# One DMA queue for loads and stores in a strided mean-subtract kernel: SyncE issues both in alternation, ScalarE none

## The chip, the cores and the metric

The kernel runs on one core of one Trainium2 chip. Time is device microseconds of the whole execution, and the states of runs are compared only where they are the same; all runs told here were of the fast state. A single-core program has no second die to compare with, so "fast" means that no run was over 1.5% above the fastest of its kernel. Shorter times are better; a difference under 2% counts as the same.

## The reference

```python
def reference(x):                      # x: 8 x 4096 x 2112, float32
    B, S, D = x.shape
    stride = 4
    x_r = x.reshape(B, S // stride, stride, D)
    pooled = x_r.mean(axis=2)
    upsampled = np.repeat(pooled, stride, axis=1)
    return (x - upsampled).astype(np.float32)
```

Each group of four rows loses its own mean. 276.8 MB are read and as many written; there is little arithmetic per byte.

## The kernel before

Four rows of 2112 numbers make one partition's row of 33,792 bytes, 128 of them a tile of 4.325 MB, and there are n = 64 tiles. Six tiles fit in SBUF (`SLOTS = 6`). SyncE issues all loads into its DMA queue, ScalarE all stores into another; VectorE adds three times and subtracts once per tile.

```python
    with tc.tile_critical():
        for k in range(n):
            b, lap = k % SLOTS, k // SLOTS
            load = nc.sync.dma_start(out=slots[b][:], in_=xg[k * P:(k + 1) * P])
            if lap:
                load._wait_ge(store_sems[b], 16 * lap)
            load.then_inc(load_sems[b], 16)

        with nc.vector.Fori(0, laps) as lap:
            landed = nc.vector.to_reg(16 * lap + 16)
            for b in range(SLOTS):
                reduce_tile(b, landed)      # three adds, one multiply-add; waits on load_sems[b]
            # ... (step semaphore wound back)
        # ... (the rest of the tiles)

        for k in range(n):
            b = k % SLOTS
            store = nc.scalar.dma_start(out=og[k * P:(k + 1) * P], in_=slots[b][:])
            store._wait_ge(done_sem, k + 1)
            store.then_inc(store_sems[b], 16)

    for k in range(n - SLOTS, n):           # closing waits on the last stores
        total = nc.gpsimd.to_reg(16 * (k // SLOTS + 1))
        tc.keep_in_program_order(nc.gpsimd.wait_ge(store_sems[k % SLOTS], total))
```

## Time and profile before

| | before |
|---|---|
| timed, median of the first 3 runs | 1284.73 us (1284.65 to 1285.19) |
| span of the profiled execution | 1283.3 us |
| VectorE busy | 1026.5 us, 80% |
| the 16 DMA engines busy | 50.1% loads + 50.0% stores of the span |
| first load landed, last store landed (semaphore records) | 13.30 and 1282.39 us |

The lines themselves, and how to read them, stand in the prediction below.

### The profile page before, as it was taken

What the parts mean: (1) busy time and instruction counts of PE and PEld (TensorE: products, weight loads), DVE (VectorE), ACT (ScalarE), POOL (GpSimd) and SP (SyncE); (2) the same over time, 40 slices, a digit from 0 to 9 for tenths busy, and PEclk for the clock granted to TensorE, in tenths of its full rate; (3) what the DMA queues carried; (4) which work ended last, traced back from release to release, by engine and by line L of the source; (5) the groups of instructions that cost most, each with busy time, mean ns of one, the idle gap of its engine ahead of it and who ended that gap; (6) DMA issues with size and microseconds to landing.
All of it is one profiled execution on the core that took longest, in us unless ns stands there. A gap on an engine that the chain in (4) does not pass through costs nothing.

```text
span 1283.3 us, 483 instructions
## 1 busy us (share of the span) xinstructions
DVE 1026.5 (80%) x256; POOL 0.2 (0%) x4
## 2 busy tenths in 40 slices
DVE  5998788787887877878778787787877878878785
POOL 0000000000000000000000000000000000000000
DMA  9999999999999999999999999999999999999999
GB/s 404 420 436 429 434 437 434 427 437 436 427 436 437 434 427 437 436 427 436 437 433 428 437 436 426 437 437 433 428 437 434 428 437 437 432 429 437 434 427 404
DMA packets 18432, 553.66 MB, mean 431 GB/s; under 512 B 2048, under 2 KB 2048, under 8 KB 2048
## 3 DMA queue, kind: packets, MB, share of 16 engines
q1 hardware_dynamic: 9216, 276.83, 50.1%
q10 hardware_dynamic: 9216, 276.83, 50.0%
HBM read 276.82 MB, written 276.82 MB: 431 GB/s over the span
## 4 chain that ended last, share of the span: by engine, by line
DVE 73%; another core or an unknown queue 24%; DMA 1%; issue 1%; DVEq 0%; SPq 0%
DVE slot L69 38%; DVE s_ps L63 18%; DVE s_sb L63 18%; DMA slot<-in_x_dram 1%; DVEq L90 0%; SPq L133 0%; SPq L82 0%
## 5 line engine op out<-in xcount | busy, mean ns | idle before, releaser
L69 DVE SCALAR_TENSOR_TENSOR slot<-s_sb,slot 128x8448 f32<-128x8448 f32 x32 | 286.7, 8958 | 1.1
L69 DVE SCALAR_TENSOR_TENSOR slot<-s_ps,slot 128x8448 f32<-128x8448 f32 x32 | 286.6, 8957 | 1.1
L63 DVE TENSOR_TENSOR s_sb<-slot 128x2112 f32<-128x2112 f32 x32 | 75.5, 2358 | 123.7 <-DMA slot<-in_x_dram 123.7
L63 DVE TENSOR_TENSOR s_ps<-slot 128x2112 f32<-128x2112 f32 x32 | 75.7, 2367 | 112.1 <-DMA slot<-in_x_dram 112.1
L63 DVE TENSOR_TENSOR s_ps<-s_ps,slot 128x2112 f32<-128x2112 f32 x64 | 151.4, 2366 | 2.2
L63 DVE TENSOR_TENSOR s_sb<-s_sb,slot 128x2112 f32<-128x2112 f32 x64 | 150.9, 2358 | 2.2
L122 POOL MEMSET const-bfloat16-1.0<- 128x1 bf16 x1 | 0.1, 102 | 0.0
L122 POOL MEMSET const-uint8-127<- 128x1 uint8 x1 | 0.1, 102 | 0.0
L122 POOL MEMSET const-float32-0.0<- 128x1 f32 x1 | 0.1, 99 | 0.2 <-issue 0.2
L122 POOL MEMSET const-float32-1.0<- 128x1 f32 x1 | 0.1, 99 | 0.0
## 6 DMA issues: line engine op xcount, KB each, us to landing
slot<-in_x_dram SPq DMA_DIRECT2D x64, 4224.0 KB, 60.1
out_dram<-slot ACTq DMA_DIRECT2D x64, 4224.0 KB, 43.5
```

The costliest lines, as they stand in the source:

```text
L63: add = nc.vector.tensor_add(out=s[:], in0=first, in1=rows[:, f, :])
L69: sub = nc.vector.scalar_tensor_tensor(out=rows, in0=s[:, None, :].to_broadcast([P, STRIDE, D]), scalar=-1.0 / STRIDE, in1=rows, op0=mybir ...
L122: nc = _bacc.Bacc("TRN2", target_bir_lowering=False, num_devices=1)
```

## The change

The intent is to have one queue whose order is fixed by the program: a load and a store in turn, so that the loads cannot crowd out the stores. Because SyncE stops at a load whose buffer is not yet free, one store more than needed (`AHEAD = 1`) is put in front of each such load, so that the queue still holds work meanwhile.

```diff
+AHEAD = 1
@@
-        for k in range(n):
+        def load_tile(k):
             b, lap = k % SLOTS, k // SLOTS
             load = nc.sync.dma_start(out=slots[b][:], in_=xg[k * P:(k + 1) * P])
             if lap:
                 load._wait_ge(store_sems[b], 16 * lap)
             load.then_inc(load_sems[b], 16)
+
+        def store_tile(k):
+            b = k % SLOTS
+            store = nc.sync.dma_start(out=og[k * P:(k + 1) * P], in_=slots[b][:])
+            store._wait_ge(done_sem, k + 1)
+            store.then_inc(store_sems[b], 16)
+
+        for k in range(SLOTS):
+            load_tile(k)
+        for k in range(n):
+            store_tile(k)
+            if k >= AHEAD and k + SLOTS - AHEAD < n:
+                load_tile(k + SLOTS - AHEAD)
@@ (the loop of stores on ScalarE is gone)
-        for k in range(n):
-            b = k % SLOTS
-            store = nc.scalar.dma_start(out=og[k * P:(k + 1) * P], in_=slots[b][:])
-            store._wait_ge(done_sem, k + 1)
-            store.then_inc(store_sems[b], 16)
```

## The prediction

> **What bounds the kernel now.** I read the page first, its parts 1 to 3, to see which resource is full; then the DMA queue's own waits, to see who holds whom; then the DMA view and the windows, to get the cost of one transfer with one queue alone and with both. The page of the kernel before:
>
> ```profile
> span 1283.3 us, 483 instructions
> DVE 1026.5 (80%) x256; POOL 0.2 (0%) x4
> ...
> DMA packets 18432, 553.66 MB, mean 431 GB/s; under 512 B 2048, under 2 KB 2048, under 8 KB 2048
> ...
> q1 hardware_dynamic: 9216, 276.83, 50.1%
> q10 hardware_dynamic: 9216, 276.83, 50.0%
> ...
> slot<-in_x_dram SPq DMA_DIRECT2D x64, 4224.0 KB, 60.1
> out_dram<-slot ACTq DMA_DIRECT2D x64, 4224.0 KB, 43.5
> ```
>
> VectorE is busy 1026.5 us, so it is idle a fifth of the time: 16.04 us of work per tile, 64 tiles. The two DMA queues take 50.1% and 50.0% of the 16 engines' whole span, together all of it. So the transfers set the end. There are 128 of them (64 loads, 64 stores) of 4224 KB, that is 128 partitions of 33,792 bytes, 4.325 MB each. The chain of waits on the page names VectorE with 73%, which must not mislead: its pieces are VectorE working while a transfer that VectorE then waits for is under way.
>
> The waits confirm it. The loads wait in SyncE for stores (the DMA queue's own waits; columns: total us, times, longest), and VectorE's idle time goes to loads (the engines' waits):
>
> ```profile
> SPq L85 <- DMA out_dram<-slot: 1169.0, 58, 50.7
> ```
>
> ```profile
> DVE s_sb L63 <- DMA slot<-in_x_dram: 123.7, 30, 13.3
> DVE s_ps L63 <- DMA slot<-in_x_dram: 112.1, 30, 3.8
> ```
>
> A load waiting in the sequencer costs nothing as long as other transfers are queued, and they are: a load takes 60.1 us from issue to landing, a store 43.5. At some 20 us for one load and one store side by side, there are always about three loads and two stores under way.
>
> Next, is the DMA slower with two queues than with one? Windows of the kernel before (columns: window and its length, VectorE and GpSimd busy with counts, clock, DMA share, GB/s), then the DMA view of a stretch in which only loads run:
>
> ```profile
> 54.78:1252.66 1197.88, 969.27 (x241) 0.00 (x0) 1.00 1.00 433
> ```
>
> ```profile
> q1 hardware_dynamic: 352, 10.81, 100.2%
> ```
>
> In the long middle, from 54.78 to 1252.66 us (the landings of the loads of tiles 3 and 63, as the semaphore records have them), 60 tiles' loads and 60 stores land: 1197.88 / 120 = 9.982 us for one transfer. In the loads-only stretch from 4 to 29 us the one queue fills the engines alone (100.2%) and moves 10.81 MB in 25 us, 433 GB/s, the same rate. The counts there are coarse, so I take landings. The first two loads land at 13.30 and 23.25 us by the semaphore records: 9.95 us between them. At the end only stores are left; the last three are issued at 1228.93, 1248.87 and 1268.88 and take 33.5, 23.5 and 13.5 us to land, so they land at 1262.4, 1272.4 and 1282.4: 9.97 to 9.98 us each. One queue alone, back to back, runs at 9.95 to 9.98 us per transfer; two queues at 9.98.
>
> **What the Trainium skill says.** "DMA: Bandwidth & Descriptors", section "Where 436 GB/s comes from", gives 435.2 GB/s as the ceiling of the 16 ports. From it I estimate 4.325 MB / 435.2 = 9.94 us as the least time of a transfer; the trace's 9.95 to 9.98 agrees and leaves 0.4% to gain at most. The same page, "Issuing engines are not separate DMA queues", says that DMAs of all issuing engines run on the same 16 engines, and that several issuers save only sequencer time. The trace agrees: one queue alone 433 GB/s, both 433. Its section "Queues, rings and completion order" says that an engine goes round-robin between queues packet by packet, and within one queue consumes in order. The trace fits: with both queues filled each has half the time. "Anatomy of one DMA — SWDGE (gpsimd) path" says that semaphore waits sit on the issuing sequencer, while the DMA engines just consume. This makes a wait at the head of one sequencer hold back everything behind it, and is what the change risks.
>
> **The change, part by part.** Bytes, transfers, VectorE's work and slots stay as they are. ScalarE's 64 issues (338 ns each in the trace) move to SyncE, whose own 64 take 328 ns: 64 x 0.338 = 21.6 us more sequencer time spread over 1283 us, beside transfers that are already queued; nothing on the path.
>
> What changes is the order. The queue now holds: six loads, store 0, store 1, load 6, store 2, load 7, and so on; load k+5 stands between stores k and k+1, and waits for store k-1 to land. I work it out with 9.96 us a transfer (the mean of 9.95 and 9.97). Loads 0 to 5 are issued within 3.9 us and land at 13.3, 23.3, 33.2, 43.2, 53.1, 63.1. Store 0 is issued when VectorE is done with tile 0, at 29.5, but stands behind load 5: it lands at 73.1, store 1 at 83.0. At 73.1 load 6 is issued, and behind it store 2 (VectorE was done with tile 2 at 61.5), while store 1 is under way. At 83.0 load 7 and store 3 (done at 77.5) follow. From then on, when store k-1 lands, load k+4 and store k are still to run: 20 us of work. Load k+5 comes with a delay of under a microsecond, and store k+1 follows it at once, if VectorE is done with tile k+1. Load k+1 landed five transfers, 50 us, before that moment; VectorE needs 16. So neither wait ever empties the queue: 20 us of reserve on the loads, some 34 on the stores.
>
> At the end load 63 is the 123rd transfer, landing at 13.3 + 122 x 9.96 = 1228.4, where it was 1252.7. VectorE is then done at about 1244.5 instead of 1268.9; stores 59 to 62 are already queued, and store 63 queues behind them.
>
> The sum: first landing 13.3 (0.95 of start and 12.35 of the first load, as now), 127 more at 9.96 = 1264.9, last landing 1278.2, plus 0.95 from the last landing (1282.4) to the end as now: span 1279.2. The timed figure is 1.4 us above the profiled span (1284.73 against 1283.3): 1280.6. Before, the same formula needs 9.993 us a transfer, for the 1269.1 us from first to last landing: 0.03 x 127, some 4 us, is all there is to win. Changing from load to store inside a ring may cost a few hundredths of a microsecond, so I say 1281.
>
> **The rivals.** First, a bubble at each change of direction: every transfer now follows one of the other kind in the same ring. If the completion of a store or the start of a load held up its successor, that would happen up to 122 times; 0.2 us each gives 24 us, 1305 and slower by nearly 2%, a full microsecond 1400. Against it: loads follow loads and stores follow stores at 9.95 to 9.98 without a bubble, and with two queues each engine already serves loads and stores in turn at 9.98. For it: no stretch of the kernel before has a load behind a store in one queue. I hold this for the main risk, about one in twenty for losses over 2%.
>
> Second, blocking at the head of SyncE: a store that is ready stands behind a load that waits. Were the reserve too short, the queue would run dry for part of 20 us per tile; 2 us per tile would make 1410. The working above leaves 20 us of reserve; the extra store ahead is there for just that. Few per cent.
>
> Third, a gain: loads come at full rate instead of in halves, so VectorE starts tile 1 on with data earlier and finishes 24 us earlier. But the end is that of the last store, and the bytes before it are the same; even at the 9.94 estimate the timed end is about 1278. Faster by 2% (under 1259) would need 442 GB/s; nothing in the trace shows it.
>
> **Range and chances.** Central 1281. The low end, 1276, is a little under 9.94 us a transfer; the high end, 1288, allows 0.06 us more per transfer than computed. Within 2%: 0.93; slower 0.05 for the first two rivals; faster 0.02.
>
> **What would show it.** One DMA queue with 18432 packets at about 100%, mean 432 to 433 GB/s with no slice under 400 beyond the first and last. Loads from 6 on take about 30 us from issue to landing (three transfers), stores about 40 (four). SyncE's waits are nearly all on stores, 58 times, close to 19.3 us each (two transfers less two issues), and hardly any on VectorE after the first two stores. VectorE's last instruction ends near 1244.5, with about the same total busy time. I am wrong if the middle shows over 10.1 us per transfer with full queues (first rival), if the DMA share falls below 97% with SyncE waiting for VectorE or for landings (second), or if the rate in the middle exceeds 436 GB/s.

## The result, and the profile after

The changed kernel took 1287.99 us (median of 5 runs, 1287.80 to 1288.35); the kernel before, in the same rounds, 1284.73 (1284.56 to 1285.19). The ratio is 1.0024, with a 95% interval of 1.0012 to 1.0037. Ratios here are the mean time of one kernel's runs over that of the other's of the same rounds, so not quite the ratio of the medians. So the time is the same within 2%, and still 3.3 us longer, clear of the noise, where the prediction's centre was nearly 4 us shorter than before.

The page of the changed kernel, the same parts as in the prediction:

```profile
span 1286.0 us, 481 instructions
DVE 1026.0 (80%) x256; POOL 0.2 (0%) x4
...
q1 hardware_dynamic: 18432, 553.66, 99.9%
...
slot<-in_x_dram SPq DMA_DIRECT2D x64, 4224.0 KB, 29.9
out_dram<-slot SPq DMA_DIRECT2D x64, 4224.0 KB, 39.5
```

One queue now carries everything and fills the engines for 99.9% of the span. A load takes 29.9 us from issue to landing (three transfers), a store 39.5 (four): the queue is as deep as worked out. What SyncE waits for (total us, times, longest us):

```profile
SPq L86 <- DMA out_dram<-slot: 1111.3, 58, 28.5
SPq L93 <- DVE slot L70: 85.5, 5, 25.7
```

The 58 waiting loads wait 19.2 us each on the average, and while they do the engines are busy. Of the five waits for VectorE, two are those of stores 0 and 1 and lie in the first 130 us (41.4 us together), and the others come at the end, where stores follow each other with no load between them and earlier stores are still queued.

So the queue is never empty, and yet time is lost. Where, the windows show (window and its length, VectorE and GpSimd busy with counts, clock, DMA share, GB/s). I cut at landings of the changed kernel: of the first load (13.36), of the fifth (53.29), and at 216.80, the landing of the 21st transfer. The changed kernel:

```profile
13.36:53.29 39.93, 39.59 (x12) 0.00 (x0) 1.00 1.00 433
53.29:216.80 163.51, 152.12 (x37) 0.00 (x0) 1.00 1.00 428
216.80:1240.00 1023.20, 823.05 (x207) 0.00 (x0) 1.00 1.00 433
```

The kernel before, in the same windows:

```profile
13.36:53.29 39.93, 39.62 (x12) 0.00 (x0) 1.00 1.00 420
53.29:216.80 163.51, 138.74 (x34) 0.00 (x0) 1.00 1.00 433
216.80:1240.00 1023.20, 823.17 (x208) 0.00 (x0) 1.00 1.00 433
```

After 217 us both run at 433 GB/s. The kernel before loses in the first window, into which its first store falls (issued at 29.5 us); the changed kernel loses in the second, where its queue first changes from loads to stores and back. The DMA share stays 1.00 in both: the engines are not idle, single rows take longer.

The trace records each row (33,792 bytes by one engine) with its start and duration. The views of the profile do not print these records; I read them from the packed trace. They do not name the engine, but in a filled queue each row starts within some 10 ns of the end of the one before it, so they can be chained into 16. Nearly every row, load or store, in both kernels takes 1251 ns. In the changed kernel the last rows of load 5, begun at 60 to 62 us, just ahead of the queue's first store, are longer: 0.92 us more per engine, mean of the 16. After that single rows are longer here and there up to about 260 us, most of them (39 of 59) the last row of a load ahead of a store, others among a load's first three; 0.84 us more on the mean, but 2.6 us on the slowest engine. In the kernel before there is one such place, at 31 to 37 us, where its first store begins, with 0.99 us per engine, and nothing after it. So both kernels pay nearly the same at their first store, with one queue or two; what one queue adds is the longer rows after it.

A transfer has landed when its slowest engine has. The 16 landings of one transfer lie within 0.43 us of each other at load 4, and within 3.2 to 3.5 us in the whole later part, where six engines follow ten by about 1.1 us or more. To compare runs I use one sum: from the first to the last landing, less 127 transfers of 9.983 us. (9.983 is the changed kernel's own pace once the losses are over: landing 27 at 276.79, landing 128 at 1285.06, 1008.27 / 101.) This "lost" time is 1269.09 - 1267.84 = 1.2 us before and 1271.70 - 1267.84 = 3.9 us after. The 2.6 us between them are the whole difference of the profiled spans (1286.0 - 1283.3 = 2.7).

### The profile page after: what moved, and what is told of

Same layout as the page of the kernel before. It is cut to its first block, busy times and chain, and to the rows that moved or that the text cites. A ratio compares the mean times of both kernels' runs of the same rounds, so it can differ in the third digit from the quotient of the medians.

```text
span 1286.0 us, 481 instructions
## 1 busy us (share of the span) xinstructions
DVE 1026.0 (80%) x256; POOL 0.2 (0%) x4
## 3 DMA queue, kind: packets, MB, share of 16 engines
q1 hardware_dynamic: 18432, 553.66, 99.9%
## 4 chain that ended last, share of the span: by engine, by line
DMA 93%; DVE 4%; SPq 1%; issue 0%
DMA out_dram<-slot 89%; DMA slot<-in_x_dram 3%; DVE slot L70 2%; DVE s_ps L64 1%; SPq L86 1%; DVE s_sb L64 1%; SPq L141 0%; SPq L83 0%
## 6 DMA issues: line engine op xcount, KB each, us to landing
slot<-in_x_dram SPq DMA_DIRECT2D x64, 4224.0 KB, 29.9
out_dram<-slot SPq DMA_DIRECT2D x64, 4224.0 KB, 39.5
```

## The experiments

Theory: the loss is a one-off. It is paid at changes from load to store inside one ring (the list of work of one queue) while the engines make that change in step (at the same moment), and fades as they drift apart; it has to do neither with waiting, nor with SyncE, nor with VectorE. Rivals: a reserve in the queue that is a little too short; SyncE as the issuer; VectorE's traffic in the same memory; a small cost on every transfer.

All my kernels have one edit in common. The closing waits stand inside the critical section and wait on constants. One run is the control for that.

**Control.**

```diff
-    for k in range(n - SLOTS, n):
-        total = nc.gpsimd.to_reg(16 * (k // SLOTS + 1))
-        tc.keep_in_program_order(nc.gpsimd.wait_ge(store_sems[k % SLOTS], total))
+        for k in range(n - SLOTS, n):      # inside the critical section
+            nc.gpsimd.wait_ge(store_sems[k % SLOTS], 16 * (k // SLOTS + 1))
```

> The changed kernel with only its closing waits on the last stores moved inside the critical section and made against constants (the form of the original closing waits is not accepted for runs of mine). Nothing in the transfers changes, so all theories expect 1288 us timed, ratio to the kernel before 1.0015 to 1.0035, span 1286.0 to 1286.6, and a spread of 3.3 to 3.5 us between the first and the last engine's landing of one transfer in the middle.

Measured: 1287.47 us, ratio 1.0025 (1.0012 to 1.0038), span of the profiled run 1285.6, a little under the expected 1286.0; lost 3.3 us; last spread 2.8, not 3.3 to 3.5. (One of the five runs took 1289.62.) The form of the closing waits does not matter. The loss and the spread differ from run to run, which the expectation had too narrow.

**No store ahead.** `AHEAD = 1` becomes `AHEAD = 0`.

> No store queued ahead of the waiting load: the order is store 0, load 6, store 1, load 7, and each load waits for the store just before it in the queue, so the queue is empty at each of 58 loads. All theories: each empty queue costs some 2.4 us (12.35 us for the first load alone against 9.98 in a filled queue), 58 x 2.4 = 139 us, so about 1425 us. The theories differ in what comes on top. Mine (a change from load to store costs up to 0.9 us on every engine that changes in step with the others, and nothing once the engines have drifted apart): an empty queue brings the engines back in step, so the cost returns at each of 58 changes, up to 50 us more, 1450 to 1480 us, and the landing spread stays under 1.5 us. Rival (the loss belongs to the first 250 us, while VectorE runs without a pause, or to warming up): nothing on top, 1420 to 1430 us.

Measured: 1515.29 us, ratio 1.1802. A load now waits for the store right before it, and SyncE cannot pass it:

```profile
q1 hardware_dynamic: 18432, 553.66, 92.3%
...
slot<-in_x_dram SPq DMA_DIRECT2D x64, 4224.0 KB, 13.8
```

A load, first in an empty queue, lands 13.8 us after its issue. That is 3.8 us more than 9.98, and the row records divide it. Lost are 228.2 us, of which 0.94 at load 5 as before. Over the 58 refills the first rows after an empty queue are longer by 33.8 us in all (0.58 each, row mean of the engines), and the last two rows ahead of the store by 77.1 - 0.94 = 76.2 us (1.31 each). What remains, 228.2 - 0.9 - 33.8 - 76.2 = 117 us, is 2.0 each in which the engines are idle. The time lies outside what either theory expected (1450 to 1480 and 1420 to 1430). Both had the idle part a little small, and mine was right that the change of direction costs again each time, but put it at 0.9 at most; it is 1.31. The 16 landings of one transfer lie 0.8 us apart on the mean from the first store on (1.7 at most, 0.7 at the last): the engines come back nearly in step at each empty queue. The rival, nothing on top, is ruled out: here slow rows last to the end of the kernel, long after VectorE has begun to pause.

**No VectorE.** Stores wait for their own loads; the result is wrong.

```diff
-            store._wait_ge(done_sem, k + 1)
+            store._wait_ge(load_sems[b], 16 * (k // SLOTS + 1))
-        (all of the VectorE loop)
```

> A wrong result on purpose: VectorE does nothing, each store waits for its own load alone and writes x back unchanged; the order in the queue is the same. My theory (the queue's change of direction alone): the same slow rows between 60 and 260 us, the same landing spread of about 3.4 us, span 1286 and ratio 1.0015 to 1.0035 as in the control. Rival (VectorE's reads and writes of the same memory slow the transfers): no slow rows, spread near 0.5 us, span about 1283, ratio 0.999 to 1.000. Both: VectorE's time is no part of the end.

Measured: 1288.02 us, ratio 1.0030 (1.0018 to 1.0043; one of the six runs took 1292.88 and lifts it), span 1286.5. The windows (without a VectorE column) show the same dip:

```profile
53.29:216.80 163.51, 0.00 (x0) 1.00 1.00 429
216.80:1240.00 1023.20, 0.00 (x0) 1.00 1.00 433
```

1.10 us per engine at the first change, 4.1 us lost, last spread 3.7. The loss is there without VectorE's work.

**All from ScalarE.** `nc.sync.dma_start` becomes `nc.scalar.dma_start` for both.

> The same single queue in the same order, but all issued by ScalarE. If one ring for both directions is what costs 3 us, ratio 1.0015 to 1.0035 as in the control, with the same slow start and spread. If it is SyncE as the issuer of stores (slower decode, or a worse queue), it is at the time of the kernel before, ratio 0.999 to 1.0005.

Measured: 1287.48 us, ratio 1.0022 (1.0007 to 1.0036); lost 3.0 us, first change 1.2 us per engine. It is not SyncE; the loss goes with the one ring. (Not tested: whole loads and whole stores in turn, but from two queues. So the ring and the order that it brings are not told apart.)

**Two stores ahead.** `AHEAD = 2`.

> Two more stores ahead of each waiting load instead of one. If the reserve of 20 us that I worked out for one store ahead is enough (my prediction's step), nothing changes: ratio 1.0015 to 1.0035. If part of the changed kernel's 3 us is a wait at the head of SyncE that a longer reserve removes, ratio 0.999 to 1.0005. Loads take about 30 us from issue to landing with one store ahead; with two, about 50, as two more transfers stand before them.

Measured: 1287.72 us, ratio 1.0029 (1.0017 to 1.0041; one of six runs took 1292.51). Loads land after 49.9 us, as worked out; lost 3.1 us. A longer reserve gains nothing, so one store ahead was enough.

**Four buffers.** `SLOTS = 4`.

> Four buffers instead of six, one store ahead as in the changed kernel. By the prediction's working the reserve of the loads (20 us) does not depend on the number of buffers, and that of the stores on VectorE shrinks from 34 to 14 us, still above zero: nothing changes, ratio 1.001 to 1.004, spread of the landings as in the control (the first change of direction comes at about 43 instead of 62 us). If the reserve is less than I think, 58 gaps of 2 us or more make 1400 us.

Measured: 1287.83 us, ratio 1.0021 (1.0007 to 1.0036). The first change of direction now comes at 40 to 44 us, and the long rows with it (1.2 us per engine); lost 3.9 us. The loss moves with the change of direction, not with the clock, and two buffers fewer cost nothing.

**Half the tiles**, in the changed kernel and in the kernel before; the results are wrong.

```diff
-    n = G // P
+    n = G // P // 2
```

> A wrong result on purpose: the changed kernel on the first 32 of the 64 tiles only. If its loss against the kernel before is a one-off of the first 250 us (my theory), it stays about 2.7 us: with the kernel before at half length near 646 us timed, this is 648.5 to 649.5. If it is a little on every transfer, it halves: 647.2 to 647.6. Span: 13.3 + 63 x 9.982 + 0.95 + 0.95 + 2.6 = about 647.

> A wrong result on purpose: the kernel before on the first 32 tiles, the partner of the half-length changed kernel. 13.3 + 63 x 9.982 + 1.6 + 0.95 = 644.7 us of span, about 646 timed, under every theory.

Measured: 648.94 and 646.04 us, a difference of 2.9 us where the full length has 3.3 (and 2.6 in the control). The lost times, with 63 transfers of 9.983, are 4.5 and 0.8 us; the profiled run of the first was the slowest of its four (649.75). A cost on every transfer would have halved: it is a one-off.

**Engines that begin late.** If being in step is what costs, engines put out of step beforehand should not pay. Short loads ahead of everything keep some of the 16 engines busy at the start; they write into the last buffer, whose own load waits for them.

```diff
+        for j in range(2):
+            late = nc.sync.dma_start(out=slots[SLOTS - 1][j * 8:(j + 1) * 8], in_=xg[j * 8:(j + 1) * 8])
+            late.then_inc(late_sem, 16)
         for k in range(SLOTS):
             load_tile(k)
@@ load_tile
+            elif b == SLOTS - 1:
+                load._wait_ge(late_sem, 32)
```

> Ahead of everything, two short loads of 8 partitions each (they are overwritten by the load of the last buffer, which waits for them), so that 8 of the 16 engines begin 2 x 1.25 = 2.5 us late. My theory (a change from load to store costs an engine only while others change with it): at the first change, near 62 us, the rows lose clearly less than the 0.92 us per engine of the changed kernel, and the scattered losses after it shrink; the late engines end 2.5 us late all the same, so the span is 1284 to 1285, ratio 0.9995 to 1.0015. Rival (the first store on an engine is dear by itself, and the later losses come with time): 0.9 us on every engine again and the scattered losses on top of the 2.5, span 1287 to 1289, ratio 1.003 to 1.005.

The next is the same with 4 in place of 8:

> The same with 4 partitions each, so 4 of the 16 engines begin 2.5 us late, much as the changed kernel ends up by itself (four engines 2 to 3.5 us behind twelve). My theory: the twelve in step lose about 0.9 us at the first change, the four late ones little, and nearly nothing is lost after that, so the span is about 1284 to 1285, ratio 0.9995 to 1.0015. Rival (every engine's first change is dear, or the loss comes with time): the four late ones lose like the rest, on top of 2.5 us: 1287 to 1289, ratio 1.003 to 1.005.

Measured: 1295.76 us (ratio 1.0084) and 1292.71 (1.0062), both outside what either theory expected. (The second expectation's picture of the changed kernel was off as well: six engines end up behind ten there, not four behind twelve.) The starts went wrong: the short loads' rows took 2.8 to 4.7 us each, and the first real load landed at 21.89 and 21.92 us instead of 13.36, 8.5 us late. The Trainium skill, "SBUF — State Buffer", section "Door 1: The DMA port swizzle (why `[64,N]` ≈ `[32,N]`)", puts partitions 0 to 3 on one port and 4 to 7 on another, so that I had sent four engines at a time through one port. In turn, four rows of 1.25 us would take 5.0 us (my estimate); rows of about 4.35 us in the second short load of the first kernel come near that. It does not explain all: in the second kernel the first real load's rows on the other twelve engines took 3.1 to 3.9 us too.

What came after the start is worth more than the times. With eight late (their landings 1.7 us behind the other eight at the first change) the first change costs nothing, but long rows come later, 3.8 us per engine between 90 and 400 us, and 4.7 us are lost in the profiled run. That run was the slowest of its five (1297.38 us); if the others started alike, they lost 2.4 to 3.7 us. With four late (by 1.8 to 3 us) there are no long rows at all, at the first change or later, and 1267.65 us pass from the first to the last landing: lost -0.2, nothing. The windows of this kernel from 68.50 us on, where the earliest engine lands its share of the sixth load and the first change from loads to stores begins, show no dip (the columns as above):

```profile
68.50:230.00 161.50, 153.78 (x41) 0.00 (x0) 1.00 1.00 433
230.00:1240.00 1010.00, 810.18 (x202) 0.00 (x0) 1.00 1.00 433
```

The kernel with eight late has its dip later:

```profile
21.89:71.00 49.11, 48.78 (x13) 0.00 (x0) 1.00 1.00 434
71.00:400.00 329.00, 285.42 (x72) 0.00 (x0) 1.00 1.00 428
400.00:1240.00 840.00, 675.12 (x169) 0.00 (x0) 1.00 1.00 433
```

So the loss does not come of one ring as such, nor with each engine's first store. But the twelve engines still in step did not pay either, which my expectation had them do.

**The same with a mended start**: partitions 4 apart, each engine on a port of its own; one row, then two.

```diff
-        for j in range(2):
-            late = nc.sync.dma_start(out=slots[SLOTS - 1][j * 4:(j + 1) * 4], in_=xg[j * 4:(j + 1) * 4])
+        for j in range(1):     # 2 in the second kernel
+            late = nc.sync.dma_start(out=slots[SLOTS - 1][j:16:4], in_=xg[j * 4:(j + 1) * 4])
```

> The two runs with late engines lost 8.5 us at their start, because rows for neighbouring partitions, written by different engines at once, took 2.6 to 4.7 us each instead of 1.25; but from the first load's landing on, the one with four late engines lost nothing. Here the start is mended: one short load of 4 partitions that lie 4 apart, so that four engines begin one row, 1.25 us, late. If a lag of 1.25 us of four engines is enough to end the losses at the changes of direction, the span is 13.3 + 1.25 + 127 x 9.982 + 0.95 = 1283.3, ratio 0.9995 to 1.0010. If it isn't enough, the first change costs 0.9 us again and losses follow: span 1285 to 1287, ratio 1.002 to 1.004. Rival (the losses are a matter of time or of each engine's first store): 1287 to 1288.

> The same with two such loads, so four engines begin 2.5 us late, about the lag that the changed kernel's four last engines reach by themselves. My theory: no losses after the first landing, span 13.3 + 2.5 + 127 x 9.982 + 0.95 = 1284.5, ratio 1.000 to 1.002. Rival: 0.9 us at the first change and the scattered losses on top, span 1287 to 1288.5, ratio 1.003 to 1.005.

Measured: 1288.67 us (ratio 1.0030, 1.0017 to 1.0044) and 1289.70 (1.0037, 1.0023 to 1.0051). The first real load landed at 15.06 and 16.89 us, so the mended partitions took away most of the bad start. The first change costs 0.98 and 0.88 us per engine again. The lags at load 4 had come out at 1.1 us in all in the one and 1.8 in the other, with no more than 0.7 us between the twelve and the four. Lost are 2.8 and 2.0 us; the full-length kernels with filled queues and no late engines lost 3.0 to 4.1, so the first is hardly less, and neither is nothing. For the second the expectation of my theory (no losses, ratio up to 1.002) failed.

| kernel | lost, us | longer rows at the first change, us per engine | after it | spread at load 4 | spread at the end |
|---|---|---|---|---|---|
| before (two queues) | 1.2 | 0.99 | 0.00 | 1.05 | 0.80 |
| changed | 3.9 | 0.92 | 0.84 | 0.43 | 3.40 |
| eight late | 4.7 | 0.00 | 3.81 | 2.12 | 4.05 |
| four late, first form | -0.2 | 0.00 | 0.02 | 3.24 | 3.21 |
| four late, one row | 2.8 | 0.98 | 0.54 | 1.09 | 2.98 |
| four late, two rows | 2.0 | 0.88 | 0.42 | 1.80 | 2.84 |

(Each row is one profiled run. For the kernel before, whose loads and stores land in pairs, "load 4" is the fifth transfer to land.) None of these versions beats the kernel before: a late engine also ends late, and what is saved in long rows is spent at the start.

## Why the prediction was right or wrong

The class and the range held, the range by luck: 1287.99 lies at its very top, 1276 to 1288, and two of the five runs (1288.24 and 1288.35) lie above it. The direction did not hold: the centre had the change faster by nearly 4 us, and it is slower by 3.3. Of the sum, mainly two terms failed, the pace of a transfer and the cost of changing direction. Point by point:

- **The bound, right.** Transfers filled the engines before and after (99.9%), and removing all of VectorE's work (1288.02 us) changed nothing.
- **Queue order and reserve, right.** Loads at 29.9 us and stores at 39.5 after issue, 58 waits of 19.2 us each, as written (30, 40, 19.3); three more waits for VectorE at the end (44.1 us) cost nothing. Two stores ahead and four buffers give the same time. The second rival, blocking at the head of SyncE, is real but not here: with no store ahead the ratio is 1.18.
- **The pace of 9.96 us, too short.** It was the mean of single distances: 9.95 between the first two landings (9.96 if the mean of the 16 engines is taken instead of the slowest), and 9.97 at the end. The working had 9.982 from 120 transfers beside them and did not use it. The pace is 9.983, in both kernels: 127 x 0.023 = 2.9 us.
- **"A few hundredths" for a change from load to store, wrong in form.** In the steady part it is zero. At the beginning it is a lump: 0.9 us on each engine at the first change, about what the kernel before pays at its first store (0.99), and up to 2.6 us more on the slowest, which is what one queue adds; 3.9 us in the sum of landings. The first rival had the place right, the changes of direction, and the form wrong, too: it would have been paid 122 times, and by the successor, where here it is mostly the last row of the load ahead that takes longer. Why it is a one-off, the runs show in part: with an empty queue at every load the engines stay in step and pay 1.31 us each time; in one run with four engines 1.8 us or more behind the rest nobody paid.
- **The 1.4 us from span to time, too small.** I had set the span of one execution of the kernel before against the median time of others. For one and the same run it is 1.8 us: 1285.12 us with a span of 1283.3 in a later round, and 1287.80 with 1286.0 for the changed kernel. That is 0.4 us.
- **The sum.** 1280.6 + 2.9 + 3.9 + 0.4 = 1287.8, against 1287.99. The same two terms move load 63 from 1228.4 to 1235.10 us, and VectorE's end from 1244.5 to 1251.3.
- **The gain of 4 us over the kernel before did not exist.** I took its 9.993 us per transfer for something that one queue would save. 9.983 of it is the common pace, and 1.2 us in all is its own single loss when stores join in, which the changed kernel pays as well.

Still open: what the engines contend for at the change, whether it is the ring or the order, and the rule by which a lag protects. "Apart by about one row" fits the changed kernel, the control and the first four-late run, but eight late engines with 1.7 us between the groups lost 3.8 us per engine in long rows, more than any other full-length run with filled queues. The first two late-engine kernels also differ in their start from the others. That fading comes from drifting apart is thus supported, not settled.

## What to carry to other kernels

With the DMA engines full and transfers of 4.3 MB, the split of loads and stores over one or two queues hardly mattered here (0.24%): find the pace of one transfer in the trace, multiply by their number, and only the start and end are left to argue about. One queue for both needs its order planned, so that transfers are still queued when something at its head has to wait: two were enough here, none cost 18%. Two queues give that for nothing. Take a pace from many landings in a steady part, never from two.

## What the Trainium skill lacked or had wrong

- "DMA: Bandwidth & Descriptors", section "Issuing engines are not separate DMA queues", says that several issuers save only sequencer time. For bandwidth this holds to 0.24% (1.0024). It does not draw the consequence for one queue that the prediction drew from another section of the page (waits sit on the issuing sequencer): with no store ahead of a waiting load the same transfers took 1515 us instead of 1285.
- No page tells that rows can take longer where loads give way to stores: 0.92 us per engine at the first change in the changed kernel and 0.84 after it, 0.99 once with two queues, 1.31 us at each of 58 refills with no store ahead, and nothing in the steady part at 9.983 us per transfer. That it hangs on the engines being in step is not settled.
- "DMA: Bandwidth & Descriptors", section "Where 436 GB/s comes from", adds that for transfers between HBM and SBUF the HBM's share of about 358 GB/s binds. Taken alone this does not hold here: with one core streaming, all kernels with filled queues ran at 433 GB/s, loads and stores together. What that sentence lacks is its condition, which the same page has in its section on measured bandwidth: about 358 GB/s is each core's share when both cores of the HBM stream. No run here had a second core.
